# A bidirectional RWKV-7 scan with VectorE's turns written out, u copied by ScalarE and products taken with the decayed state, and attention's value products issued in one row

## The chip, the cores and the metric

The kernel runs on one core of a Trainium2 chip. A core has five engines that each work through their own list of instructions in order: TensorE (PE in the profile) for matrix products, VectorE (DVE), ScalarE (ACT), GpSimd (POOL) and SyncE (SP), which here issues most of the DMA transfers. They meet by semaphores. The metric is the device time of one execution in microseconds (us), lower is better. Before the change it is 1709.98 us, the median of three runs from 1708.64 to 1715.86.

## The reference

One encoder layer over 1024 tokens with a model width of 1024. The part that matters is this (shapes are noted behind):

```python
proj = rms_norm(x) @ w_in                      # q, k, v | r, k, v, ... of the time mix | branch gates
attn = windowed_gqa(q, k, v, sink)             # blocks of 128 queries, up to 3 key blocks each, 2 kv heads x 4 q heads
def step(state, inp):                          # time mix: two directions, 8 heads, state 64 x 64
    sa = einsum('dbhij,dbhj->dbhi', state, a_t)
    state = state * w_t[..., None, :] + sa[..., :, None] * b_t[..., None, :] + v_t[..., :, None] * k_t[..., None, :]
    y = einsum('dbhij,dbhj->dbhi', state, r_t)
rw = groupnorm(y_forward + flip(y_backward)) ...
merged = gate0 * (attn @ w_up_attn) + gate1 * (rw @ w_up_rwkv)
x = x + merged @ w_out
x = x + square(relu(rms_norm(x) @ w_ff1)) @ w_ff2
x = x + (p @ w_ple) * sigmoid(rms_norm(x) @ w_ple_gate)
```

All of it is float32. Where the kernel wants float32 accuracy from faster products it splits both operands into a high and a low part and takes three products (high by high, low by high, high by low); `split` (L197, L198) makes the parts: ScalarE casts the high one, VectorE subtracts for the low one.

## The kernel before

The program runs in stages: input projection and preparation (to about 340 us), attention (about 340 to 486 us), the scan (about 486 to 800 us), the epilogue and the branches' up products (to about 907 us), output projection, the two feed-forward products and the gated embedding.

**Attention** takes the 1024 queries in 8 tiles n of 128. For each tile and each of 2 kv heads it computes scores `sc`, a softmax, transposes the probabilities (`pt`, copied into `pT`), and at last the value products `po` (L956): for each key block j and each kv head, one product whose 64 output columns lie in that head's half of the array. Tiles 1 to 6 have three key blocks and so six products, tiles 0 and 7 two and four. Here, TensorE's order among independent work is left to the scheduler. Work of the input projection for the gates (`gmm`) fills TensorE between these products.

**The scan** is chunked: the 1024 tokens are 16 chunks of 64, and step s handles chunk s forward and chunk 15-s backward at once. Within a chunk the recurrence needs the inverse of a unit lower triangular matrix per head and direction; the kernel computes these inverses for blocks of NB = 4 steps together, one block ahead of their use. So inverse b (b = 1, 2, 3) is worked on during steps 4(b-1) to 4b-1. Its parts are:

- `low_products`: four parts (ci = 0 to 3), one for each chunk of the block, each 32 small products `lps` from loaded tiles `la` and `lb`, copied to `lt`. Loads of part ci+1 are issued when part ci has been computed.
- `inverse`: four ScalarE copies into `Lc` (1024 columns by 32 partitions each), a transposition `Lp` on VectorE, and 31 elimination steps of two VectorE operations each (`tmp`, a product, and `Z`, an addition).
- `inverse_turned`: two more transpositions `Zn` and `Zt`, and `inverse_off`: products `qps`, copies `Q`, and the off-diagonal part; the results go into `zi`.

Step s itself runs on TensorE in a fixed order (every product goes through `mmo`, L220, or is pinned): `carried(s)`, products of the operands with the state of step s-1 into `wy`; products for s+2 (`gps`, masked by VectorE into `gm`); `u_part`: `ups` = inverse by W, and next to it `wa` for the next step; `s_part`: `sps`, the contribution to the state; `y_part`: the outputs, again into `wy`; `operands(s+1)`: transpositions `tmps`, copied by ScalarE to `tm`. Eight gaps are filled with projection products (`gmm`) in steps 0 to 13, and `aside(i)` takes part i of the next inverse's low products in steps 0, 4 and 8. From step 12 on, the epilogue is mixed in.

The other engines' share of a step: u has 64 rows for each direction, on two halves of the partitions. VectorE copies the first half out of `ups` into `UV`, ScalarE the second (L1212, L1213). `W` of the next step is copied from `wa` by ScalarE (L1192) and VectorE adds the carried part (L1199). VectorE adds `sps` to the decayed old state (`S`, L1225) and decays it for the next addition (`Sc`, L1230). The state that `carried` multiplies is the undecayed `S`; the decay is put into the operands instead: `decayed` lets ScalarE scale the tiles `ra` in place, eight operations a step (L1164).

Only TensorE's order is fixed by hand. On VectorE and ScalarE a scheduler sets the order of the scan's work, so the elimination steps of the inverse stand wherever it placed them between `UV`, `W`, `gm`, `S`. DMA issues on SP stand in one list too: among them `g_d` (a gate tile that ScalarE has just made, `gth`, stored), `la` and `lb`, and, from step 11 on, `atl` and `wust` (attention's output and the weights that lift it), whose parts `aTh`, `aTl`, `wuhi`, `wulo` feed `uaps`.

Of the kernel before, what the change touches and what calls it, by code (L numbers as in the profile page):

```python
# [17 lines left out]
P = 128  # L18
# [6 lines left out]
NP = 4  # L25
# [38 lines left out]
LEAD = 1  # L64
FILLQ = 8

LOW_AT = 3
# [77 lines left out]
def block_kernel(ctx: ExitStack, tc: tile.TileContext, I: dict, out: bass.AP):  # L145
# [629 lines left out]
    def low_products(pl, ps_of, b, mm, behind=None):  # L775
# [14 lines left out]
        for ci in range(NB):  # L790
            la, lb = nxt
            pss = [ps_of([P, NP, 64], "lps") for _ in range(2)]
            for j in range(NP):
                for q in range(2):
                    for d in range(ND):
                        e = q ^ d
                        rows = slice(64 * e, 64 * e + 64)
                        l_, r_ = (lb, la) if d == 0 else (la, lb)
                        mm(pss[e][own[d], j, :], l_[d][rows, j, :], r_[d][rows, j, :], start=True, stop=True)
            for e in range(2):  # L800
                nc.scalar.copy(lt[:, 8 * ci + e:8 * ci + 8:2, :], pss[e])
            if ci + 1 < NB:
                nxt = load(ci + 1)
            yield lt
# [84 lines left out]
    with ExitStack() as s2:  # L889
# [21 lines left out]
        for n in range(NT):  # L911
# [42 lines left out]
            for j in range(nk):  # L954
                for kv in range(2):
                    nc.tensor.matmul(po[kv * 64:kv * 64 + 64], V[:, k0 + j, kv * 64:kv * 64 + 64], pTs[kv][:, j, :, :], start=(j == 0), stop=(j == nk - 1))  # L956
# [152 lines left out]

    ch_tm, ch_uv, ch_S, ch_wy, Sc = {}, {}, {}, {}, {}  # L1110

# [9 lines left out]
    def products(s, hf):  # L1121
# [14 lines left out]
        for e in range(2):  # L1136
            nc.vector.tensor_tensor(
                out=gm[hf][:, s % NB, e].rearrange("p (a b) t -> p a b t", b=2), in0=pss[e][:, 0:6].rearrange("p (a b) t -> p a b t", b=2),
                in1=gmask.unsqueeze(2).broadcast_to([P, 3, 2, 64]), op=ALU.mult)

# [17 lines left out]

    def decayed(s):

        for d in range(ND):
            for j in range(NP):
                r_ = ra_t[s % NRA, d][:, j, :]
                nc.scalar.activation(out=r_, in_=r_, func=AF.Copy, scale=Dt[:, d, j, s - 1:s])  # L1164

    def w_own(s, h, wa):
# [28 lines left out]
    def w_sum(s, W):  # L1195

        if s > 0:
            for e in range(2):
                nc.vector.tensor_tensor(out=W[:, e::2, :], in0=W[:, e::2, :], in1=ch_wy[s][e][:, 0:4, :], op=ALU.add)  # L1199

    def u_part(s, W):

        up = PB.tile([P, NH, 64], F32, name="ups", tag="us", bufs=1)
        nxt = s + 1 < NCH
        wa = wa_tile() if nxt else None
        for h in (0, 2, 4, 6, 1, 3, 5, 7):
            for d in range(ND):
                mmo(up[own[d], h, :], zi[own[d], 8 * (s % NB) + h, :], W[own[d], h, :], start=True, stop=True)
            if nxt:
                w_own(s + 1, h, wa)  # L1210
        UV = ch_uv[s]
        nc.vector.tensor_copy(UV[own[0], 0], up[own[0]])  # L1212
        nc.scalar.copy(UV[own[1], 1], up[own[1]])  # L1213
        return w_copy(wa) if nxt else None

    state = [None]

    def s_part(s):
        sp = PB.tile([P, ND, NP, 64], F32, name="sps", tag="us", bufs=1)
        for d in range(ND):  # L1220
            for h in range(NH):
                mmo(sp[own[h % 2], d, h // 2, :], ch_tm[s, d][:, h, :], ch_uv[s][:, d, h, :], start=True, stop=True)
        S = ch_S[s] = B.tile([P, ND, NP, 64], F32, name="S", bufs=2)
        if s > 0:
            nc.vector.tensor_tensor(out=S, in0=sp, in1=Sc.pop(s - 1), op=ALU.add)  # L1225
        else:
            nc.vector.tensor_copy(S, sp)
        if s < NCH - 2:
            Sc[s] = B.tile([P, ND, NP, 64], F32, name="Sc")
            state[0] = nc.vector.tensor_tensor(out=Sc[s], in0=S, in1=Dt[:, :, :, s].unsqueeze(3).broadcast_to([P, ND, NP, 64]), op=ALU.mult)  # L1230

    def y_part(s):
# [8 lines left out]
        for e in range(2):  # L1241
            yo = yv[:, e::2, c0:c1 + 1:c1 - c0, :]
            yp = ch_wy[s][e][:, 4:8, :].rearrange("q (d a) t -> q a d t", d=2)
            if s < NCH // 2:
                nc.scalar.copy(yo, yp)
            else:
                for d in range(ND):
                    nc.vector.tensor_tensor(out=yo[:, :, 1 - d], in0=yo[:, :, 1 - d], in1=yp[:, :, d], op=ALU.add)

    def low(b):  # L1250

        if b in lows:
            lts[b] = next(lows[b])

# [35 lines left out]
    for s in range(NCH):  # L1290
# [8 lines left out]
        def aside(i):  # L1299

            b = s // NB + 1
            if b < NCH // NB and (s % NB, i) in ((0, 0), (0, 1), (0, 2), (0, 3)):
                low(b)
                if i == 3:
                    zzs[b] = inverse(BI, lts[b])
            if ep is not None:
# [639 lines left out]
```

## Time and profile before

The profiled execution took 1708.72 us, 1.3 us less than the median; its span is 1706.9 us, so 1.8 us lie around the span.

| what | value |
|---|---|
| time, median of 3 (range) | 1709.98 us (1708.64 to 1715.86) |
| profiled execution, span | 1708.72 us, 1706.9 us |
| TensorE busy in the span | 1622.9 us, 95% |
| VectorE, ScalarE busy | 1146.3 us (67%), 869.2 us (51%) |
| attention, 340 to 486 us: TensorE, VectorE busy | 130.55 us, 103.34 us of 146 |
| scan, 486 to 800 us | 16 steps |

The busy shares of the whole span say little of the scan: there TensorE has gaps, and these are read from the waits. In the lists of waits the first name is the waiting operation, the name behind the arrow what it waited for; then follow the total in us, how often, and the longest. In the timelines the columns are start, duration, engine, line, operation, result and operands, and in brackets the idle time before with what ended it. Line L220 is the helper through which nearly all of the scan's products go, so the scan is read by tile names.

### The profile page before, as it was taken

To read this page: it belongs to the slowest core of one execution; us is meant where nothing else is said; L and a number is where in the kernel's file an instruction comes from. 1 tells how busy PE (TensorE), PEld (TensorE's weight loads), DVE (VectorE), ACT (ScalarE), POOL (GpSimd) and SP (SyncE) were. 2 spreads that over 40 slices of the span, in tenths; PEclk is the share of its full clock that TensorE was granted. 3 is DMA by queue.
4 is the path that set the end of the run, shared out by engine and by line. 5 is a ranking of instruction groups with operands and counts; after the bars stand their busy time and mean duration, and the time that the engine had idled before them with its cause. 6 is when DMAs were issued, how large, how long until landed. Compare 5 with 4: busy or idle time off the path is not lost.

```text
span 1706.9 us, 31260 instructions
## 1 busy us (share of the span) xinstructions
PE 1622.9 (95%) x12280; PEld 1310.1 (77%) x12280; DVE 1146.3 (67%) x2071; ACT 869.2 (51%) x1605; POOL 102.6 (6%) x113
## 2 busy tenths in 40 slices
PE   7999999989998988798999999999999999999998
PEld 7987777756567777676778878888888888888887
DVE  6658998165957596866764787676667867685342
ACT  5548887367645646565422454444444444544221
POOL 3430000411200000000000000000000000000000
PEclk9999999989999999899999999999999999999999
DMA  6353566755356544546762144444439865474110
GB/s 220 81 153 106 161 182 179 226 162 143 99 162 175 158 150 138 174 126 210 240 216 86 62 159 155 142 154 151 162 129 345 281 217 155 158 219 149 43 40 37
DMA packets 200835, 269.24 MB, mean 158 GB/s; under 512 B 47728, under 2 KB 103920, under 8 KB 200688
## 3 DMA queue, kind: packets, MB, share of 16 engines
q1 hardware_dynamic: 190752, 254.14, 47.0%
q0 software_dynamic: 9792, 12.59, 2.8%
q8 instruction: 96, 1.57, 0.4%
q10 hardware_dynamic: 144, 0.52, 0.1%
q14 instruction: 51, 0.42, 0.1%
HBM read 186.45 MB, written 80.74 MB: 157 GB/s over the span
## 4 chain that ended last, share of the span: by engine, by line
PE 72%; DVE 13%; DMA 7%; ACT 4%; issue 3%; POOL 1%; SPq 1%; DVEq 0%; ACTq 0%; POOLq 0%
PE ff1ps L1575 16%; PE ff2ps L1827 16%; PE gmm L220 2%; PE uaps L220 2%; DVE Z L824 2%; DVE tmp L821 2%; PE plps L230 2%; PE plps L228 2%; PE plps L226 2%; PE mm L238 2%; PE po L956 2%; PE mm L240 2%; PE mm L239 2%; DMA wst<-in_w_col_dram 1%; PE sc L927 1%
## 5 line engine op out<-in xcount | busy, mean ns | idle before, releaser
L1827 PE MATMUL ff2ps<-tl,sh 128*128 128x512 f32 x448 | 174.5, 390 | 0.2 <-DVE tl L198 0.2
L1827 PE MATMUL ff2ps<-th,sl 128*128 128x512 f32 x448 | 174.4, 389 | 0.0
L1827 PE MATMUL ff2ps<-th,sh 128*128 128x512 f32 x448 | 173.9, 389 | 0.0
L197 ACT CAST sh<-sst 128x512 fp32r<-128x512 f32 x109 | 67.8, 622 | 105.0 <-PE ff2ps L1827 49.4
L198 DVE TENSOR_TENSOR sl<-sst,sh 128x512 fp32r<-128x512 f32 x109 | 75.1, 689 | 46.4 <-ACT sh L197 46.3
L1575 PE MATMUL ff1ps<-mh,w1h 128*128 128x512 f32 x256 | 100.3, 392 | 1.9 <-ACT w1h L197 1.9
L1575 PE MATMUL ff1ps<-ml,w1h 128*128 128x512 f32 x256 | 99.9, 390 | 0.0
L1575 PE MATMUL ff1ps<-mh,w1l 128*128 128x512 f32 x256 | 99.6, 390 | 0.0
L1827 PEld LDWEIGHTS ff2ps<-tl,sh 128*128 128x128 f32 x448 | 84.1, 188 | 18.4 <-DVE tl L198 0.8
L1827 PEld LDWEIGHTS ff2ps<-th,sh 128*128 128x128 f32 x448 | 84.0, 188 | 17.8 <-ACT th L197 0.3
L1827 PEld LDWEIGHTS ff2ps<-th,sl 128*128 128x128 f32 x448 | 84.1, 188 | 17.3
L197 ACT CAST whi<-wst 128x512 fp32r<-128x512 f32 x100 | 60.2, 616 | 63.5 <-DMA wst<-in_w_col_dram 29.2
L197 ACT CAST w1h<-w1st 128x512 fp32r<-128x512 f32 x48 | 28.3, 620 | 95.2 <-DMA w1st<-in_w_ff_dram 58.3
L182 POOL TENSOR_TENSOR rstd<-ms,neghalf 128x1 f32<-128x1 f32 x24 | 14.8, 617 | 1029.1 <-DVE pp L198 573.1
L198 DVE TENSOR_TENSOR w1l<-w1st,w1h 128x512 fp32r<-128x512 f32 x48 | 31.7, 687 | 50.5 <-ACT w1h L197 50.5
L198 DVE TENSOR_TENSOR wlo<-wst,whi 128x512 fp32r<-128x512 f32 x72 | 48.2, 687 | 21.1 <-ACT whi L197 20.9
L226 PE MATMUL gmm<-hh,whi 128*128 128x512 f32 x136 | 56.7, 417 | 3.3 <-ACT whi L197 3.3
L1575 PEld LDWEIGHTS ff1ps<-mh,w1h 128*128 128x128 f32 x256 | 48.0, 188 | 12.9 <-ACT w1h L197 2.8
L1575 PEld LDWEIGHTS ff1ps<-mh,w1l 128*128 128x128 f32 x256 | 48.1, 188 | 10.8 <-DVE w1l L198 0.6
L228 PE MATMUL gmm<-hl,whi 128*128 128x512 f32 x136 | 56.2, 413 | 0.0
L1575 PEld LDWEIGHTS ff1ps<-ml,w1h 128*128 128x128 f32 x256 | 48.1, 188 | 10.0
L230 PE MATMUL gmm<-hh,wlo 128*128 128x512 f32 x136 | 55.6, 410 | 0.0
(397 smaller groups left out, 4585.4 us busy)
## 6 DMA issues: line engine op xcount, KB each, us to landing
wst<-in_w_col_dram SPq DMA_DIRECT2D x92, 256.0 KB, 3.4
tst<-in_w_ff_dram SPq DMA_DIRECT2D x80, 256.0 KB, 4.0
w1st<-in_w_ff_dram SPq DMA_DIRECT2D x32, 512.0 KB, 4.9
hid_S<-h SPq DMA_DIRECT2D x64, 256.0 KB, 2.1
sst<-hid_S SPq DMA_DIRECT2D x64, 256.0 KB, 3.1
hid_A<-h SPq DMA_DIRECT2D x48, 256.0 KB, 2.2
sst<-hid_A SPq DMA_DIRECT2D x45, 256.0 KB, 3.6
ra_d<-ra SPq DMA_DIRECT2D x8, 1024.0 KB, 5.7
```

What stands on the lines that cost most here:

```text
L197: a = nc.scalar.copy(hi, src)
L198: b = (lo_eng or nc.vector).tensor_tensor(out=lo, in0=src, in1=hi.bitcast(F32), op=ALU.subtract)
L220: tc.keep_in_program_order(nc.tensor.matmul(*a, **kw))
L226: mm(ps, ah, bh, start=(i == 0), stop=False)
L228: mm(ps, ah, bl, start=False, stop=False)
L230: mm(ps, al, bh, start=False, stop=(i == n - 1))
L238: nc.tensor.matmul(ps, ah, bh, start=(i == 0), stop=False)
L239: nc.tensor.matmul(ps, ah, bl, start=False, stop=False)
L240: nc.tensor.matmul(ps, al, bh, start=False, stop=(i == n - 1))
L821: nc.vector.tensor_tensor(out=tv, in0=Lp[:, t + 1:32, t:t + 1].broadcast_to([P, n, m]), in1=Z[:, t:t + 1, 0:m].broadcast_to([P, n, m]), op ...
L1575: nc.tensor.matmul(ps, x_[:, k, :], y_[:, k, :], start=start and k + i == 0, stop=k == 3 and i == 2, skip_group_check=True)
L1827: nc.tensor.matmul(banks[bs][i], x_[:, isl], y_, start=fresh and p + j == 0, stop=p == NPR - 1 and j == 2, skip_group_check=True)
```

## The change

It has five parts.

1. **Turns.** The scheduler no longer sets the order of VectorE's own scan work. `turn` pins each of these operations to the place where the program issues it: the mask products `gm`, the additions to `W`, `S`, `Sc`, `y`, and the operations of the inverse, which is now a generator (`inverse_steps`) advanced by `inverse_turn(n)`. `TURNS` gives the number of elimination steps at three places of each of the four steps of a block. What `split` issues (`wlo`, `aTl`, `wulo`, `rwl`) is not pinned, and neither is ScalarE's work.
2. **u** is copied out of `ups` by ScalarE alone, both halves.
3. **Decay.** `decayed` is gone; `carried` multiplies the decayed state `Sc` with the operands as loaded. In step 0 no copy of the state is made; `Sc` is taken from `sps`.
4. **Low products.** The copies into `Lc` are made part by part after each `lt` (32 partitions by 256 columns, sixteen for an inverse, instead of four of 1024 columns), and the fourth part, `aside(3)`, is moved from the end of the step (behind gap 7) to just behind gap 4, in steps 0, 4 and 8; the order of directions within a part is turned round.
5. **Attention.** The order of the two kv heads in the value products is turned round: the head whose probabilities are ready last goes first.

The core of the diff:

```diff
+TURNS = ((0, 0, 4), (3, 2, 5), (3, 2, 5), (4, 3, 1))
...
-                    for d in range(ND):
+                    for d in (1, 0):
...
-                for kv in range(2):
+                for kv in (1, 0):
                     nc.tensor.matmul(po[kv * 64:kv * 64 + 64], V[:, k0 + j, kv * 64:kv * 64 + 64], pTs[kv][:, j, :, :], start=(j == 0), stop=(j == nk - 1))
...
+    def turn(ins):
+        tc.keep_in_program_order(ins)
...
-    def decayed(s):
-
-        for d in range(ND):
-            for j in range(NP):
-                r_ = ra_t[s % NRA, d][:, j, :]
-                nc.scalar.activation(out=r_, in_=r_, func=AF.Copy, scale=Dt[:, d, j, s - 1:s])
...
-            S = ch_S[s - 1]
+            S = Sc[s - 1]
...
-        nc.vector.tensor_copy(UV[own[0], 0], up[own[0]])
-        nc.scalar.copy(UV[own[1], 1], up[own[1]])
+        for d in range(ND):
+            turn(nc.scalar.copy(UV[own[d], d], up[own[d]]))
...
-        S = ch_S[s] = B.tile([P, ND, NP, 64], F32, name="S", bufs=2)
+        S = sp
         if s > 0:
-            nc.vector.tensor_tensor(out=S, in0=sp, in1=Sc.pop(s - 1), op=ALU.add)
-        else:
-            nc.vector.tensor_copy(S, sp)
-        if s < NCH - 2:
-            Sc[s] = B.tile([P, ND, NP, 64], F32, name="Sc")
-            state[0] = nc.vector.tensor_tensor(out=Sc[s], in0=S, in1=Dt[:, :, :, s].unsqueeze(3).broadcast_to([P, ND, NP, 64]), op=ALU.mult)
+            S = B.tile([P, ND, NP, 64], F32, name="S", bufs=1)
+            turn(nc.vector.tensor_tensor(out=S, in0=sp, in1=Sc.pop(s - 1), op=ALU.add))
+        Sc[s] = B.tile([P, ND, NP, 64], F32, name="Sc", bufs=2)
+        turn(nc.vector.tensor_tensor(out=Sc[s], in0=S, in1=Dt[:, :, :, s].unsqueeze(3).broadcast_to([P, ND, NP, 64]), op=ALU.mult))
...
+    def low(b, ci):
+
+        lt = lts[b] = next(lows[b])
+        if ci == 0:
+            Lcs[b] = BI.tile([P, 32, 32], F32, name="Lc", tag="inv", bufs=3)
+        for r0 in range(0, P, 32):
+            k = r0 // 32 % 2
+            nc.scalar.copy(Lcs[b][r0:r0 + 32, 8 * ci:8 * ci + 8], lt[r0:r0 + 32, 8 * ci:8 * ci + 8, 32 * k:32 * k + 32])
...
+    def inverse_steps(b):
+
+        Lc = Lcs.pop(b)
+        Lp = BI.tile([P, 32, 32], F32, name="Lp", tag="inv", bufs=3)
+        turn(nc.vector.transpose(out=Lp, in_=Lc.rearrange("s p t -> s t p")))
...
+        for t in range(31):
+            n, m = 31 - t, t + 1
+            tv = tmp[:, 0:n * m].rearrange("p (n m) -> p n m", m=m)
+            turn(nc.vector.tensor_tensor(
+                out=tv, in0=Lp[:, t + 1:32, t:t + 1].broadcast_to([P, n, m]),
+                in1=Z[:, t:t + 1, 0:m].broadcast_to([P, n, m]), op=ALU.mult))
+            turn(nc.vector.tensor_tensor(out=Z[:, t + 1:32, 0:m], in0=Z[:, t + 1:32, 0:m], in1=tv, op=ALU.add))
+            yield
+        Zn = BI.tile([P, 32, 32], F32, name="Zn", tag="inv", bufs=3)
+        Zt = BI.tile([P, 32, 32], F32, name="Zt", tag="inv", bufs=3)
+        turn(nc.vector.transpose(out=Zn.rearrange("r p c -> r c p"), in_=Z.rearrange("p r c -> p c r")))
+        turn(nc.vector.transpose(out=Zt.rearrange("c p r -> c r p"), in_=Z))
+        zzs[b] = Zn, Zt, None
+
+    inv = [iter(())]
+
+    def inverse_turn(n):
+        for _ in range(n):
+            next(inv[0], None)
...
         gap(0)
         aside(0)
+        inverse_turn(TURNS[s % NB][0])
         gap(1)
         W = u_part(s, W)
-        if nxt:
-            decayed(s + 1)
         if more:
             products(s + 2, 1)
+        inverse_turn(TURNS[s % NB][1])
         gap(2)
         gap(3)
         aside(1)
         if nxt:
             s_part(s)
         y_part(s)
-        if s % NB == NB - 1 and s // NB < 3:
-            b = s // NB + 1
-            zzs[b] = inverse_turned(BI, zzs[b], state[0])
         aside(2)
         gap(4)
+        if s % NB == 0 and s // NB < 3:
+            aside(3)
+            inv[0] = inverse_steps(s // NB + 1)
+        inverse_turn(TURNS[s % NB][2])
         gap(5)
...
-        aside(3)
+        if s % NB or s // NB >= 3:
+            aside(3)
```

How this moves instructions is shown at three places. The first is TensorE in step 4, at the low products of block 2: `lps` are these products, `gmm` the filler, `tmps` the transpositions of the next step's operands. Before, from the last product of the third part to the first of the fourth:

```order
L220 MATMUL lps<-lb,la 64x64
L220 MATMUL gmm<-hh_90,wlo 128x512
L220 MATMUL gmm<-hh_90,whi 128x512
L220 MATMUL gmm<-hl_91,whi 128x512
...
L1154 MATMUL tmps<-ident,bkc_4614 128x128 x4
L1154 MATMUL tmps<-ident,bkc_4618 128x128 x4
...
L220 MATMUL gmm<-hh_90,wlo 128x512
L220 MATMUL lps<-la,lb 64x64
```

and now:

```order
L221 MATMUL lps<-la,lb 64x64
L221 MATMUL gmm<-hh_90,wlo 128x512
L221 MATMUL gmm<-hh_90,whi 128x512
L221 MATMUL gmm<-hl_91,whi 128x512
L221 MATMUL lps<-lb,la 64x64
```

Of the ten `gmm` and eight `tmps` that stood between the two parts, three `gmm` are left; the other seven and the `tmps` come behind the fourth part.

The second place is ScalarE in step 11, the last step before the epilogue. `gth` is the gate tile, `rac` are the tiles that `decayed` scales, `aTh` and `wuhi` high parts of loaded tiles. Before:

```order
L328 ACTIVATE gth<-gmm 128x512
L1192 COPY W<-wa 128x512
L1213 COPY UV<-ups 64x512
L1164 ACTIVATE rac_3037<-rac_3037,Dt 128x128 x2
L1164 ACTIVATE rac_3040<-rac_3040,Dt 128x128 x2
L197 CAST aTh<-atl 128x512 x2
L1156 COPY tm<-tmps 128x512
L197 CAST wuhi<-wust 128x512
L1156 COPY tm<-tmps 128x512
L197 CAST wuhi<-wust 128x512
```

and now:

```order
L329 ACTIVATE gth<-gmm 128x512
L1190 COPY W<-wa 128x512
L198 CAST aTh<-atl 128x512 x2
L198 CAST wuhi<-wust 128x512 x2
L1211 COPY UV<-ups 64x512 x2
L198 CAST aTh<-atl 128x512 x2
L198 CAST wuhi<-wust 128x512
```

The copies of u, which stood ahead of the casts of loaded tiles, now stand behind four of them.

The third place is VectorE in the same step. `tmp` and `Z` are the elimination steps of the inverse (the last three of them are left out at the mark), `aTl` and `wulo` low parts of the loaded tiles, `gm` the masked products. Before, where the elimination had ended ahead of the step:

```order
L1137 TENSOR_TENSOR gm_4610<-gps,gmask 128x384 x2
L1225 TENSOR_TENSOR S<-sps,Sc 128x512
L1230 TENSOR_TENSOR Sc<-S,Dt 128x512
L198 TENSOR_TENSOR aTl<-atl,aTh 128x512
...
L198 TENSOR_TENSOR wulo<-wust,wuhi 128x512
L198 TENSOR_TENSOR wulo<-wust,wuhi 128x512
L831 STREAM_TRANSPOSE Zn<-Z 128x32x32
```

and now:

```order
L199 TENSOR_TENSOR wulo<-wust,wuhi 128x512 x2
L1267 TENSOR_TENSOR tmp<-Lp,Z 128x175
L1270 TENSOR_TENSOR Z<-Z,tmp 128x7x25
...
L199 TENSOR_TENSOR wulo<-wust,wuhi 128x512
L1270 TENSOR_TENSOR Z<-Z,tmp 128x5x27
...
L1142 TENSOR_TENSOR gm_4610<-gps,gmask 128x384 x2
...
L1222 TENSOR_TENSOR S<-sps,Sc 128x512
...
L1224 TENSOR_TENSOR Sc<-S,Dt 128x512
...
L1274 STREAM_TRANSPOSE Zn<-Z 128x32x32
```

Seven elimination steps, the second `gm`, `S`, `Sc`, `y` and `Zn` now stand behind `aTl` and `wulo`, three of the latter among them.

More of the change, by code (lines that the diff above doesn't have):

```diff
@@ L1198, in w_sum @@
             for e in range(2):
[L1199 removed]
+                turn(nc.vector.tensor_tensor(out=W[:, e::2, :], in0=W[:, e::2, :], in1=ch_wy[s][e][:, 0:4, :], op=ALU.add))
     def u_part(s, W):
@@ L1247, in y_part @@
                 for d in range(ND):
[L1248 to L1253, printed above, removed]
+                    turn(nc.vector.tensor_tensor(out=yo[:, :, 1 - d], in0=yo[:, :, 1 - d], in1=yp[:, :, d], op=ALU.add))
+    Lcs = {}
+    def low(b, ci):
[9 more added lines that the diff above has]
+        turn(nc.vector.transpose(out=Lp, in_=Lc.rearrange("s p t -> s t p")))
+        Z = BI.tile([P, 32, 32], F32, name="Z", tag="inv", bufs=3)
+        nc.gpsimd.memset(Z, 0.0)
+        nc.gpsimd.memset(Z.rearrange("p r c -> p (r c)")[:, ::33], 1.0)
+        tmp = BI.tile([P, 256], F32, name="tmp", bufs=1)
+        for t in range(31):
+            n, m = 31 - t, t + 1
+            tv = tmp[:, 0:n * m].rearrange("p (n m) -> p n m", m=m)
+            turn(nc.vector.tensor_tensor(
+                out=tv, in0=Lp[:, t + 1:32, t:t + 1].broadcast_to([P, n, m]),
[11 more added lines that the diff above has]
+            next(inv[0], None)
     def begin_low(b):
@@ L1302, in aside @@
             if b < NCH // NB and (s % NB, i) in ((0, 0), (0, 1), (0, 2), (0, 3)):
-                low(b)
-                if i == 3:
-                    zzs[b] = inverse(BI, lts[b])
+                low(b, i)
             if ep is not None:
```

6 lines of the change are left out of this document (2 added, 4 removed).

## The prediction

> **What bounds the kernel now.** I read the page first, then the busy times by stage, then TensorE's waits in the scan, and last the timelines around the longest of them.
>
> ```profile
> span 1706.9 us, 31260 instructions
> PE 1622.9 (95%) x12280; PEld 1310.1 (77%) x12280; DVE 1146.3 (67%) x2071; ACT 869.2 (51%) x1605; POOL 102.6 (6%) x113
> ```
>
> TensorE sets the time; outside it only 84 us are left. The change leaves its products as they are, so it can win only idle time, or time in which an array half stands empty. Where is the idle time?
>
> ```profile
> 430.00:475.00 45.00, 40.77 (x198) 25.32 (x196) 40.90 (x139) 29.83 (x82) 8.73 (x7) 1.00 0.27 82
> 475.00:600.00 125.00, 114.42 (x2601) 93.62 (x2601) 76.48 (x155) 69.15 (x151) 2.22 (x4) 0.97 0.62 175
> 527.00:537.00 10.00, 6.75 (x83) 5.94 (x82) 9.59 (x27) 5.17 (x12) 0.00 (x0) 0.83 0.58 142
> 600.00:720.00 120.00, 99.50 (x2340) 82.26 (x2340) 97.31 (x230) 63.58 (x139) 1.11 (x2) 0.97 0.50 151
> 707.00:717.00 10.00, 4.03 (x120) 3.75 (x116) 8.92 (x14) 6.88 (x13) 0.00 (x0) 0.74 0.86 259
> 720.00:800.00 80.00, 69.44 (x1134) 52.73 (x1133) 53.29 (x101) 43.66 (x79) 0.00 (x0) 0.92 0.51 161
> ```
>
> Columns: stretch, length, busy TensorE, weight loads, VectorE, ScalarE, GpSimd, granted clock, DMA share, GB/s. From 475 to 800 us TensorE lacks 10.6 + 20.5 + 10.6 = 41.7 us of 325. VectorE is nearly full exactly where TensorE is emptiest. The waits from 486 to 910 us:
>
> ```profile
> PE sps L220 <- ACT UV L1213: 13.8, 8, 3.3
> PE qps L220 <- ACT aTh L197: 6.0, 1, 6.0
> PE wy L220 <- DVE y L1248: 2.2, 4, 0.7
> PE ups L220 <- DVE W L1199: 1.8, 5, 0.5
> PE lps L220 <- DMA lb<-bk_d: 1.5, 1, 1.5
> PE gps L220 <- DVE gm L1137: 0.4, 1, 0.4
> ```
>
> The largest is `sps` on u. In step 5 it looks so (VectorE, ScalarE, TensorE):
>
> ```profile
> 602.17 0.30 DVE L824 TENSOR_TENSOR Z<-Z,tmp 128x135 f32<-128x135 f32 x1
> 602.38 0.68 DVE L1212 COPY UV<-ups 64x512 f32<-64x512 f32 x1
> 603.09 0.58 ACT L1213 COPY UV<-ups 64x512 f32<-64x512 f32 x1 [3.78 <-DVE UV L1212]
> 771.83 1.15 PE L220 MATMUL sps<-UV,tm 128*64 128x64 f32 x32 [1.69 <-ACT UV L1213]
> ```
>
> VectorE's half of u stands behind five elimination steps, and ScalarE's half starts only when VectorE's has ended. ScalarE had stood idle for 3.78 us.
>
> **The change part by part.** The sum is made against the profiled execution, 1708.7 us (1.3 below the median).
>
> *Waits in steps 1 to 10.* With both halves of u on ScalarE no elimination step stands ahead of them; two copies take 2 x 0.58 us against 0.68 + 0.58 in series now. Of the 13.8 us, 1.69 lie at 772 us (the last row above) and 0.40 in step 11 (below); 11.7 us go. Of the waits on `W`, `y` and `gm` (1.8 + 2.2 + 0.4 = 4.4) I take 0.6 as lying behind step 10; 3.8 go, since `turn` puts `W`, `gm` and `y` ahead of the elimination steps. Together **-15.5**. The cover is ScalarE, which also loses the scaling of `ra`:
>
> ```profile
> L1164 ACT ACTIVATE rac<-rac,Dt 128x128 f32<-128x128 f32 x120 | 38.9, 392 | 25.1 <-PE gps L220 24.7
> L811 ACT COPY Lc<-lt 32x1024 f32<-32x1024 f32 x12 | 12.5, 1045 | 0.2
> ```
>
> That is 38.9 us over 15 steps, 2.6 a step, off a half-busy engine: by itself worth nothing on TensorE, but it keeps u's copies, `tm` and `gth` from queueing. The twelve `Lc` copies become 48 of a quarter's width. No row has that shape; between a quarter of 1045 ns and the 0.58 us of u's 512 columns I take 0.37, 1.5 us a part, still hidden, since ScalarE is at 55% (69.15 of 125); uncovered, 48 x 0.37 less the 12.5 of now would be 5 us.
>
> *VectorE as pacemaker.* Pinning does not shorten VectorE's other work, so what TensorE no longer waits for in u it can meet elsewhere.
>
> ```profile
> L821 DVE TENSOR_TENSOR tmp<-Lp,Z 128x252 f32<-128x252 f32 x6 | 2.5, 422 | 0.2
> L1225 DVE TENSOR_TENSOR S<-sps,Sc 128x512 f32<-128x512 f32 x14 | 9.6, 686 | 4.6 <-PE sps L220 4.6
> L1137 DVE TENSOR_TENSOR gm<-gps,gmask 128x384 f32<-128x384 f32 x62 | 32.3, 550 | 15.2 <-PE gps L220 15.2
> L1248 DVE TENSOR_TENSOR y<-y,wy 128x128 f32<-128x128 f32 x32 | 7.7, 281 | 0.4 <-PE wy L220 0.4
> 706.84 1.10 PE L220 MATMUL wy<-gm,UV 128*64 128x64 f32 x32
> 707.88 1.09 PE L1154 MATMUL tmps<-ident,bkc 128*128 128x128 f32 x8
> ```
>
> Between `sps` and the next `W`, VectorE now has `S`, `Sc` (2 x 0.69) and five elimination steps (10 x 0.42 in the middle of an inverse), 5.6 us. TensorE has meanwhile `wy` of the outputs 1.1, `tmps` 1.1, the carried products (32 of the same kind, 1.1) and ten fillers, whose rows start 0.24 us apart (587.02 and 587.26 in the next fence): 5.7. So it is about even: some 0.3 us of wait a block. In steps 3 and 7 `Zn` (2.0) stands behind the last elimination step, `S`, `Sc` and (step 7) four `y` of 0.28, with `qps` behind it; there I take 1.1 and 1.4 us. With half a microsecond in step 10 this is about **+4**, with 0 and +6 as ends.
>
> *The fourth part of the low products.* It moves ahead, but its loads do not:
>
> ```profile
> 588.11 0.62 SPq L782 DMA_DIRECT2D lb<-bk_d  x1
> 587.02 0.40 PE L220 MATMUL gmm<-hh,whi 128*128 128x512 f32 x1
> 587.26 0.40 PE L220 MATMUL gmm<-hl,whi 128*128 128x512 f32 x1
> 591.91 0.24 PE L220 MATMUL lps<-lb,la 64*64 64x64 f32 x1 [1.50 <-DMA lb<-bk_d]
> ```
>
> In step 4 the last load is issued at 588.11, behind the store of `g_d`, and its product starts at 591.91 after 1.50 us of waiting; two products of the part had run by then, so TensorE had come to it at about 590.1. After the change it comes right behind the `gmm` of 587.26, at about 587.5: 2.6 us earlier. ScalarE makes `gth`, hence the store and the loads, perhaps 0.7 us sooner (a group of `rac` of 1.3 us gone, 0.58 of u come). In step 4 this makes a wait of about 3.4 us. Each of the three blocks waits 2.6 - 0.7 = 1.9 us more: **+5.6** (ends: 0, if the loads come as much earlier as the products; +7.8 if not at all). In step 4 a wait stands there already, so nothing absorbs it.
>
> *Step 11.* Here the queues decide.
>
> ```profile
> 708.59 1.24 ACT L197 CAST aTh<-atl 128x512 fp32r<-128x512 f32 x2 [1.48 <-DMA atl<-at_d]
> 711.50 0.62 ACT L197 CAST wuhi<-wust 128x512 fp32r<-128x512 f32 x1
> 712.15 0.69 DVE L198 TENSOR_TENSOR wulo<-wust,wuhi 128x512 fp32r<-128x512 f32 x1 [0.22 <-ACT wuhi L197]
> 712.76 2.04 DVE L831 STREAM_TRANSPOSE Zn<-Z 128x1024 f32<-128x1024 f32 x1
> 705.86 1.15 PE L220 MATMUL sps<-UV,tm 128*64 128x64 f32 x32 [0.40 <-ACT UV L1213]
> 714.94 3.62 PE L220 MATMUL qps<-Zn,lt 32*32 32x32 f32 x128 [5.97 <-ACT aTh L197]
> 713.26 0.53 SPq L1000 DMA_DIRECT2D wust<-in_w_up_attn_dram  x1
> ```
>
> Now `Zn` already stands behind two `aTl` and two `wulo`, and `qps` waits 5.97 us, until `Zn` ends at 714.8 (the listed releaser had long ended). After the change u's copies stand behind `aTh` x2 and `wuhi` x2: they start at 712.1, not 704.5; `sps` at 713.3, not 705.9. On VectorE seven elimination steps, `gm`, `S`, `Sc` and `y` stand behind loaded tiles too, the third `wulo` among them, whose `wust` is issued at 713.26 now and may land at 715 to 716 if it is issued sooner. From a third `wulo` ending at 717: nine elimination operations of 0.2 to 0.3 (2.4), two `gm` 1.1, `S` and `Sc` 1.4, four `y` 1.1, `Zn` 2.0 make 725, against 714.8. Operations on VectorE overlap a little (`Zn` starts at 712.76, while `wulo` of 712.15 is listed to 712.84), for which I take off 0.8: **+9.4**; ends 0 (tiles landed before they are asked for) and +11.
>
> *Steps 12 to 15*: the 1.69 us on u at 772 us may go, u may queue behind other casts: **-1** (0 to -1.7).
>
> *Attention.* The value products:
>
> ```profile
> 381.82 1.07 PE L956 MATMUL po<-pT,V 128*64 128x512 f32 x2
> 391.02 2.79 PE L956 MATMUL po<-pT,V 128*64 128x512 f32 x10
> ```
>
> The profile counts each product twice. The first of six stands alone, 1.07 us with half the array empty; the five others alternate halves and take three slots, 2.79. With the head order turned round, all six come when the last probabilities are there, in three slots: 1.07 us less in each of 8 tiles, 8 us at most. Filler covers the first while TensorE is full; in the last three tiles VectorE (40.90 of 45) limits, and the product's early place was itself free filler. Five tiles at 1 us: **-5** (0 to -8).
>
> Sum: -15.5 + 4 + 5.6 + 9.4 - 1 - 5 = **-2.5**, so 1706.2 in the profiled execution's terms, **1707.5** as a median.
>
> The granted clock adds a doubt: around the longest wait on u, 3.3 us in step 1, it was 0.83 from 527 to 537, and 0.74 around step 11. The Trainium skill's page "TensorE: Matmul & The Clock Gate", section "What's actually happening", says that about 3.4 us of idle time halve the clock; the trace agrees in direction. By it, the wait of step 4 would be at the limit and cost a stretch at half speed besides, while the one in step 1 costs none any more; by the row, which shows less than full speed after 3.3 us already, the two cancel, and the sum stays.
>
> **The rivals.**
>
> *Queues win (slower).* If step 11 costs its full 11, the loads gain nothing (+7.8), VectorE takes 6 and attention gives 1: -15.5 + 6 + 7.8 + 11 - 1 - 1 = +7.3; a clock of 0.83 over 10 us behind two waits of 3.5 us takes 1.7 each, +10.7: 1720.7. It is one mechanism, work tied to late DMA placed ahead of work that TensorE needs, in step 11 and at the low products, and it decides once both together cost over 20 us. For: the 5.97 us wait is already of this kind. Against: it needs nearly every end at once.
>
> *Step 11 mild (faster).* If the tiles land as soon as the casts ask, the 9.4 falls to 0: -11.9, 1698. For: DMA share is only 0.50 to 0.62 before. Against: it is 0.86 from 707 to 717, and the loads stand behind `g_d` in SP's list as before.
>
> *Attention gains in full, VectorE is no bound (faster)*: -15.5 + 5.6 + 9.4 - 1 - 8 = -9.5, 1700.5.
>
> *No effect of pinning*, the scheduler's order having been nearly as good: only attention and step 11 count, +4, 1714. Against: five elimination steps in front of u are in the trace.
>
> **How the numbers follow.** Less than 0.5%, 8.5 us, can't be told from no change here. My sum, within that, has a chance of 0.43, pinning without effect 0.07: same 0.50. Step 11 mild 0.20 and attention in full 0.12: faster 0.32. Queues 0.18: slower. The range, 1694 to 1719, reaches below the mild case by 4 and just to the slow one.
>
> **What would show it.** Right: `sps` waits for `UV` no more in steps 1 to 10; `ra` scaling gone; `lps` waits of 2 to 4 us on `lb` in steps 0, 4, 8; `sps` and `qps` of step 11 late by 7 and 10 us. Wrong: `sps` of step 11 without a wait, `W` or `Zn` waits over 6 us in sum, `po` still in four slots, or attention's end moved by nothing.

## The result and the profile after

The changed kernel takes 1697.3 us (median of 11 runs, 1694.52 to 1704.26), the kernel before 1709.98 us in the same number of runs. The ratio is 0.9933, 95% interval 0.9915 to 0.995: faster by 0.5 to 0.85%. That is 12.7 us, where 2.5 were forecast; the time lies in the stated range, and on the side to which I had given a chance of 0.32. Among the experiments below four single executions, of 3211 to 8857 us, stand far outside all others; the ratios leave them out, the medians hold them.

The first lines of the page after, and windows of the changed kernel (stretch, length, busy TensorE, weight loads, VectorE, ScalarE, GpSimd, granted clock, DMA share, GB/s):

```profile
span 1694.4 us, 31186 instructions
PE 1615.2 (95%) x12280; PEld 1311.1 (77%) x12280; DVE 1138.1 (67%) x2055; ACT 847.0 (50%) x1537; POOL 103.1 (6%) x113
```

```profile
430.00:475.00 45.00, 41.99 (x243) 28.65 (x241) 44.60 (x139) 31.49 (x86) 8.78 (x7) 1.00 0.30 97
517.00:527.00 10.00, 10.00 (x189) 8.29 (x190) 9.14 (x24) 4.02 (x8) 0.00 (x0) 1.00 0.71 186
527.00:537.00 10.00, 10.00 (x233) 8.08 (x233) 9.62 (x24) 4.45 (x8) 0.00 (x0) 1.00 0.65 205
600.00:720.00 120.00, 101.53 (x2454) 84.60 (x2456) 89.35 (x200) 52.85 (x103) 1.11 (x2) 0.90 0.47 143
686.00:696.00 10.00, 2.87 (x78) 2.74 (x79) 4.78 (x10) 4.73 (x8) 0.00 (x0) 0.79 0.81 252
696.00:706.00 10.00, 3.46 (x62) 3.02 (x60) 9.05 (x23) 4.50 (x8) 0.00 (x0) 0.67 0.61 198
```

The clock times of the two kernels don't match, since step 1 now comes 7 us and step 11 some 12 to 17 us earlier. The hole of step 1, at 527 to 537 before, is closed: from 517 to 537 TensorE is busy all the time, at full clock. The hole of step 11, at 707 to 717 before, lies at 686 to 706 now and has grown: TensorE is busy for 6.3 of these 20 us. TensorE's waits from 486 to 910 us in the changed kernel:

```profile
PE lps L221 <- DMA lb<-bk_d: 8.8, 3, 4.0
PE sps L221 <- ACT UV L1211: 7.4, 2, 6.6
PE uaps L221 <- ACT aTh L198: 5.5, 2, 4.8
PE qps L221 <- DVE Zn L1274: 4.9, 1, 4.9
PE tmps L1159 <- DVE gm L1142: 1.6, 1, 1.6
PE ups L221 <- DVE W L1197: 0.3, 1, 0.3
```

The eight waits of `sps` on u have become two, of 6.6 us in step 11 and 0.8 behind it; those on `W`, `y` and the scan's `gm` have gone but for 0.3 on `W` and the one of step 11. In their place the low products wait 8.8 us for `lb`, in steps 0, 4 and 8 (2.70, 2.13 and 3.95 us); before it was 1.5 us in step 4, and in step 8 0.8 us that the profile calls issue, a wait for nothing that it shows.

Where the time went is read from one product that both kernels have in every step, the first `sps`. In the kernel before, steps 0, 10, 12 and 14 (start, duration, engine, line, names):

```profile
512.57 0.34 PE L220 MATMUL sps<-UV,tm 128*64 128x64 f32 x4
693.56 0.28 PE L220 MATMUL sps<-UV,tm 128*64 128x64 f32 x2 [1.68 <-ACT UV L1213]
735.90 0.28 PE L220 MATMUL sps<-UV,tm 128*64 128x64 f32 x2
771.83 0.28 PE L220 MATMUL sps<-UV,tm 128*64 128x64 f32 x2 [1.69 <-ACT UV L1213]
```

and after the change:

```profile
503.69 0.28 PE L221 MATMUL sps<-UV,tm 128*64 128x64 f32 x2
676.59 0.28 PE L221 MATMUL sps<-UV,tm 128*64 128x64 f32 x2
723.32 0.28 PE L221 MATMUL sps<-UV,tm 128*64 128x64 f32 x2
757.90 0.28 PE L221 MATMUL sps<-UV,tm 128*64 128x64 f32 x2 [0.83 <-ACT UV L1211]
```

| stretch | before | after | difference | forecast |
|---|---|---|---|---|
| start to `sps` of step 0 (attention in it) | 512.57 | 503.69 | -8.9 | -5 |
| step 0 to step 10 | 180.99 | 172.90 | -8.1 | -5.9 (-15.5 + 4 + 5.6) |
| step 10 to step 12 (step 11 in it) | 42.34 | 46.73 | +4.4 | +9.4 |
| step 12 to step 14 | 35.93 | 34.58 | -1.4 | -1 |
| step 14 to the span's end | 935.1 | 936.5 | +1.4 | 0 |
| span | 1706.9 | 1694.4 | -12.5 | -2.5 |

Up to step 14 every stretch moved the way it was forecast; three sizes were off. One execution of each kernel was profiled, and among the runs below those with the same program in a stretch differ by up to 4.9 us ahead of step 0 (503.85 and 508.71), up to 5.5 us in steps 0 to 10 (172.9 and 178.4) and up to 1.9 us from step 10 to step 12 (46.7 and 48.6), so a smaller difference between two runs is not shown by its stretch alone.

In step 11 the queues did what the order had shown. VectorE, with rows left out at the marks:

```profile
690.76 0.69 DVE L199 TENSOR_TENSOR aTl<-atl,aTh 128x512 fp32r<-128x512 f32 x1 [4.58 <-ACT aTh L198]
...
692.40 1.45 DVE L199 TENSOR_TENSOR wulo<-wust,wuhi 128x512 fp32r<-128x512 f32 x2
693.77 0.33 DVE L1267 TENSOR_TENSOR tmp<-Lp,Z 128x175 f32<-128x175 f32 x1
...
697.50 0.68 DVE L199 TENSOR_TENSOR wulo<-wust,wuhi 128x512 fp32r<-128x512 f32 x1
...
701.28 0.68 DVE L1222 TENSOR_TENSOR S<-sps,Sc 128x512 f32<-128x512 f32 x1
...
703.39 2.05 DVE L1274 STREAM_TRANSPOSE Zn<-Z 128x1024 f32<-128x1024 f32 x1
```

VectorE stands idle for 4.58 us at the first `aTl`, with seven elimination steps behind it that need nothing from it. ScalarE does the same with u:

```profile
690.12 0.62 ACT L198 CAST aTh<-atl 128x512 fp32r<-128x512 f32 x1 [2.50 <-DMA atl<-at_d]
691.75 1.37 ACT L198 CAST wuhi<-wust 128x512 fp32r<-128x512 f32 x2
693.03 1.17 ACT L1211 COPY UV<-ups 64x512 f32<-64x512 f32 x2
```

### The profile page after: what moved, and what is told of

It reads as the page before. It is cut to its first block, busy times and chain, and to the rows that moved or that the text cites. A ratio compares the mean times of both kernels' runs of the same rounds, so it can differ in the third digit from the quotient of the medians.

```text
span 1694.4 us, 31186 instructions
## 1 busy us (share of the span) xinstructions
PE 1615.2 (95%) x12280; PEld 1311.1 (77%) x12280; DVE 1138.1 (67%) x2055; ACT 847.0 (50%) x1537; POOL 103.1 (6%) x113
## 4 chain that ended last, share of the span: by engine, by line
PE 74%; DVE 11%; DMA 6%; ACT 4%; issue 3%; POOL 1%; SPq 0%; DVEq 0%; ACTq 0%; POOLq 0%
PE ff2ps L1856 17%; PE ff1ps L1604 16%; PE gmm L221 4%; PE uaps L221 2%; PE plps L231 2%; PE plps L229 2%; PE plps L227 2%; PE mm L239 2%; PE mm L241 2%; PE mm L240 2%; PE gps L221 1%; DMA wst<-in_w_col_dram 1%; DMA g1t<-g_d 1%; PE mmo L241 1%; PE mmo L239 1%
```

## The experiments

Eleven kernels were run. A time is the median of its runs, a ratio that to the kernel before, with its 95% interval; "the change" is 0.9933 (0.9915 to 0.995).

**Attention's row alone.** The kernel before with this edit:

```diff
-                for kv in range(2):
+                for kv in (1, 0):
```

> The kernel before with one edit: the order of the two kv heads in attention's value products. In the trace of the change the scan's first product that waits for VectorE's mask stands at 476.6 us against 484.5, so theory A (the row of six saves a slot of about 1 us in all 8 tiles) expects -8 us, a ratio of 0.995, and TensorE's waits on smk falling from 5.0 to about 1.5. The rival, my prediction's term (five tiles, the rest hidden behind VectorE), expects -5 us and the waits unchanged or longer.

Measured: 1706.29 us, 0.9975 (0.9955 to 0.9994). TensorE's waits in attention in this run:

```profile
PE sc L927 <- DVE mx L928: 4.0, 6, 1.3
PE pt L948 <- DVE smk L945: 2.2, 4, 0.8
```

The value products of a tile now run in one row. In the changed kernel, which has the same edit (the profile counts each product twice):

```profile
403.42 2.79 PE L957 MATMUL po<-pT,V 128*64 128x512 f32 x12
```

All six take the 2.79 us that five took before, and the 1.07 us of the first one alone are gone. With this edit alone, too, no tile has a separate first product left. The time falls by 4.3 us (1 to 8), and the scan's first `qps` starts at 485.1 us against 490.3: 5 us, the prediction's size, not theory A's 8. The `smk` waits fall from 5.0 to 2.2, as theory A had it, but waits on `mx`, another of VectorE's operations, rise from 0.9 to 4.0: VectorE takes back part of what TensorE saves. The other direction gives more:

**The change without attention's row.** Only that line put back.

> The changed kernel with the old order of the kv heads in the value products. By the kernel before with the new order alone (about 5 us at the scan's start) the time rises by 5 us, to 1702; if the order of the products is what makes all 8 us at the scan's start, by 8, to 1705. If the pins on gm at the scan's start make the missing 3 us, the first qps stands 3 us earlier than in the kernel before (487 against 490.3).

Measured: 1706.72 us, 0.9976 (0.9958 to 0.9993), 9.4 us above the change. The first `qps` starts at 489.0 us, close to the kernel before, so the pins make little of the 8 us at the scan's start (482.2 against 490.3). By `sps` of step 0 the row is worth 10.5 us here (514.2 against 503.7) and 5.9 in the kernel before (506.7 against 512.6). Whether the row gains 4 or 9 us the intervals do not settle: both hold 3 to 8.

**u on ScalarE alone.** The kernel before, with the scheduler's order and this edit:

```diff
-        nc.vector.tensor_copy(UV[own[0], 0], up[own[0]])
-        nc.scalar.copy(UV[own[1], 1], up[own[1]])
+        for d in range(ND):
+            nc.scalar.copy(UV[own[d], d], up[own[d]])
```

> The kernel before with both halves of u copied by ScalarE, VectorE's order left to the scheduler. Theory B (u's copy behind elimination steps is the whole loss of steps 1 to 10) expects the 13.8 us of sps waits on u to fall under 2, and -10 to -12 us, ratio 0.993. The rival (VectorE is the pacemaker, its order must be pinned for it) expects waits on W, gm and y to grow by what u loses: -2 to -4 us, ratio 0.998 to 0.999.

Measured: 1710.39 us, 1.0002 (0.9982 to 1.0022): no gain. The waits of this run from 486 to 910 us:

```profile
PE ups L220 <- DVE W L1199: 4.6, 3, 2.1
PE wy L220 <- issue: 4.2, 3, 2.3
PE gmm L220 <- issue: 3.6, 1, 3.6
PE wy L220 <- DVE y L1248: 2.9, 3, 2.2
```

The waits on u fall from 13.8 to 1.4 us. Waits on VectorE's results take part of their place (`W` from 1.8 to 4.6, `y` from 2.2 to 2.9, `S` from nothing to 1.8), and so do waits called issue; steps 0 to 10 take 183.8 us, against 181.0 before. The profiled execution took 1716.66 us, 6.3 above the median, so these sums may be on the high side. Theory B falls: removing the largest wait alone gains nothing, because TensorE then waits for other things, the next results of VectorE first.

**The change without its pins.** `turn` returns without pinning; all else stays. The diff passes u's two copies on ScalarE through `turn` as well, so these are pinned in the changed kernel, and here they are not.

```diff
     def turn(ins):
-        tc.keep_in_program_order(ins)
+        return ins
```

> The changed kernel with only the pins on VectorE and ScalarE taken away; the program issues everything in the same places. If the pins carry the gain of steps 1 to 10, elimination steps go ahead of W and gm again and the waits on W, y, gm come back: +4 to +8 us against the change, ratio to the kernel before 0.996 to 0.998. If the moves alone carry it: within 2 us of the change, ratio 0.993.

Measured: 1702.14 us, 0.9945 (0.9923 to 0.9966), 4.8 us above the change. The stretches tell more than the sum. In this run steps 0 to 10 take 184.3 us (`sps` at 505.0 and 689.3), 11.4 more than in the change, with waits on `Sc`, `y`, `Z` and `W` in them; but step 10 to step 12 takes 37.8 us, 8.9 less than in the change. The fixed order gains 11.4 us up to step 10 and gives 8.9 of it back in step 11. There, without pins, ScalarE copies u at 702.0 us, ahead of the first cast at 704.2, and `sps` waits 0.3 us, so the wait of 6.6 us is gone with the pins. A kernel with pins on VectorE alone was not run.

**u by halves, pinned.** The change with u's first half on VectorE again.

```diff
-        for d in range(ND):
-            turn(nc.scalar.copy(UV[own[d], d], up[own[d]]))
+        turn(nc.vector.tensor_copy(UV[own[0], 0], up[own[0]]))
+        turn(nc.scalar.copy(UV[own[1], 1], up[own[1]]))
```

> The changed kernel with u's first half copied by VectorE again, pinned at its place. If it is the queue on VectorE that made u late, and not the engine, the pinned copy stands ahead of the elimination steps of its step and waits at most for those pinned before it: sps waits of 0 to 1 us a step, the time 0 to 5 us above the change, 1697 to 1702. If the engine matters (VectorE as pacemaker has 0.7 us a step less): 7 to 11 us above, 1704 to 1708.

Measured: 1702.65 us, 0.9964 (0.995 to 0.9977), 5.4 us above the change, at the edge of the first case. The longest wait lies in step 11 (TensorE, then VectorE and ScalarE):

```profile
706.17 1.97 PE L221 MATMUL sps<-UV,tm 128*64 128x64 f32 x32 [14.92 <-ACT UV L1211]
704.83 0.68 DVE L1210 COPY UV<-ups 64x512 f32<-64x512 f32 x1
705.54 0.58 ACT L1211 COPY UV<-ups 64x512 f32<-64x512 f32 x1 [2.18 <-DVE UV L1210]
```

`sps` waits 14.92 us there, and the four others of its waits make 4.2 together, 2.5 of them in steps 1 to 10, where they were 11.7 in the kernel before. Steps 0 to 10 take 174.7 us against 172.9. So where VectorE's order is fixed, its half of u costs hardly 2 us over ten steps: u was late by its place in the queue far more than by its engine. The long wait of step 11 is mostly made good behind it, since step 10 to step 12 takes 49.0 us against 46.7. Where the rest of the 5.4 us lies, these stretches don't settle.

**The decay put back.** The change with `decayed` and the undecayed state again:

```diff
+    def decayed(s):
...
-            S = Sc[s - 1]
+            S = ch_S[s - 1]
...
+        if nxt:
+            decayed(s + 1)
```

> The changed kernel with the decay put back into the operands: ScalarE scales ra (2.6 us a step), and the carried products use the undecayed state. My prediction held the scaling to be worth nothing by itself: within 2 us of the change. The rival: ra operations stand ahead of u's copies and gth on ScalarE, sps waits for u come back at 0.5 to 1 us a step and the lps waits grow by 0.7 each: 1702 to 1708.

Measured: 1703.01 us, 0.9964 (0.9949 to 0.998), 5.7 us above the change. By the time that is the rival's case, though the waits of `sps` in steps 1 to 10 did not come back; I had called the scaling worth nothing by itself. It costs 5.7 us, though ScalarE is half idle. Where, the traces show less surely: steps 0 to 10 take 176.7 us against 172.9, no more than single executions scatter; the `lps` waits are 10.3 us against 8.8, and `sps` of step 11 waits 8.5 us against 6.6. Both hang on ScalarE's list, `lb` by the store of `gth` ahead of its load, so the likely reason is that the scaling stands ahead of what TensorE waits for.

**The low products put back.** The fourth part, the inverse's start and its first four elimination steps at the end of steps 0, 4 and 8 again:

```diff
-        if s % NB == 0 and s // NB < 3:
-            aside(3)
-            inv[0] = inverse_steps(s // NB + 1)
-        inverse_turn(TURNS[s % NB][2])
+        if s % NB or s // NB >= 3:
+            inverse_turn(TURNS[s % NB][2])
...
-        if s % NB or s // NB >= 3:
-            aside(3)
+        aside(3)
+        if s % NB == 0 and s // NB < 3:
+            inv[0] = inverse_steps(s // NB + 1)
+            inverse_turn(TURNS[s % NB][2])
```

> The changed kernel with the fourth part of the low products, and with it the inverse's start and its first four elimination steps, put back to the end of steps 0, 4 and 8. Theory C (the earlier place costs what my sum said) expects the lps waits on lb to fall from 8.8 us to about 2.5 and the time by 5 to 6 us: ratio 0.990. The rival (VectorE starts the inverse later and TensorE waits for W behind it instead) expects W waits of 1 to 2 us in each of steps 1, 5, 9 and the time within 2 us of the change: ratio 0.993.

Measured: 1699.02 us, 0.9925 (0.9897 to 0.9953): the same as the change. The 8.8 us of waits on `lb` are gone, and this stands in their place:

```profile
PE ups L221 <- DVE W L1197: 7.1, 4, 3.0
```

In step 1 of this run `W` is added at 520.8 us, behind `Lp`, which starts at 516.6, and four elimination steps. The earlier place costs its wait and saves this one. As a price of the move, +5.6 was right for the wait and left out the other side.

**Loads two parts ahead, and casts later.** Two edits that take away the two losses, each alone and both together, on the changed kernel. First the loads, with six buffers instead of four:

```diff
...
-        nxt = load(0)
+        nxt = [load(0)] if behind else [load(0), load(1)]
...
-            la, lb = nxt
+            la, lb = nxt.pop(0)
+            if not behind and ci + 2 < NB:
+                nxt.append(load(ci + 2))
...
```

> The changed kernel with la and lb loaded two parts ahead instead of one (six buffers each instead of four), so that the last loads stand ahead of g_d in SP's list. Theory C (the 8.8 us of lps waits on lb are lost time) expects them to go and -6 to -9 us against the change, about 1690. The rival, which the run with the low products put back speaks for (VectorE is the pacemaker in the steps behind), expects waits on W or gm to take their place: within 3 us of the change.

Measured: 1696.89 us, 0.992 (0.9896 to 0.9945), the same as the change. The scan's waits on `lb` are gone, and 2.1 us of `tmps` on `lt` have come in their place: steps 0 to 10 take 166.0 us against 172.9. But in its profiled execution the scan's first `qps` came 3.7 us and step 0's `sps` 5 us later than in the change, and step 10 to step 12 took 1.9 us more. The delay ahead of step 0 is scatter: the run with both edits has the same program up to there and does not show it. Second, the tiles of attention's up products are asked for later:

```diff
         for h in range(2):
             hs = slice(512 * h, 512 * h + 512)
+            if h == 0:
+                for _ in range(17):
+                    yield 1
...
-                for _ in range(BRIDGE):
+                for _ in range(BRIDGE - 17):
```

> The changed kernel with attention's output tiles and the first up weights (atl, wust and their parts) asked for 17 filler places later in the program, nothing else; on ScalarE u of step 11 then stands ahead of their casts, on VectorE the elimination, S, y and Zn ahead of wulo. Theory D (these parts, queued ahead, cost step 11 its time) expects the waits of sps (6.6 us) and tmps (1.6) of step 11 to go and qps to be reached about 8 us earlier, of which uaps gives some back because its parts come later: -4 to -8 us against the change, 1690 to 1693. The rival (step 11 is bound by the landing of those tiles whatever stands in the queues) expects uaps to wait for what sps and qps no longer wait for: within 2 us of the change.

Measured: 1695.14 us, 0.9911 (0.9888 to 0.9935): 2.2 us below the change, within the intervals and less than the 4 to 8 expected. From step 10 to step 12 it takes 40.1 us, against 46.7 in the change and 42.3 before: u's wait there falls from 6.6 to 0.5 and that of `tmps` is gone, `qps` waits 6.2 us instead of 4.9, and `uaps` does not wait more (4.8 us in all against 5.5). In the profiled execution 4 us were lost between steps 3 and 4, among others 2.8 in a wait called issue. The rival's reading, that the landing of the tiles bounds step 11, falls.

**Both edits together.**

> Both edits together: the deeper loads and the later casts. If the two gains are separate, they add: -10 to -15 us against the change, 1682 to 1687. If VectorE's work between step 8 and Zn of step 11 is the bound, no more than the larger of the two, about 1690.

Measured: 1686.54 us, 0.9859 (0.9836 to 0.9881), 10.8 us below the change and clear of it, as expected if the gains add: the whole is 1.4% faster than the kernel before. Steps 0 to 10 take 167.5 us, step 10 to 12 38.7. Its waits:

```profile
PE qps L221 <- DVE Zn L1279: 5.3, 1, 5.3
PE uaps L221 <- ACT aTh L198: 4.1, 2, 3.4
PE tmps L1164 <- ACT lt L804: 2.1, 3, 0.7
PE sps L221 <- ACT UV L1216: 1.2, 2, 0.8
```

By the stretches the two gains add (5.4 and 8.0 us); by the medians each alone shows less than its stretch, 0.4 and 2.2 us, and why, the four runs of each leave open.

**Zn ahead of S.** On this kernel, the last of `qps`' waits:

```diff
-TURNS = ((0, 0, 4), (3, 2, 5), (3, 2, 5), (4, 3, 1))
+TURNS = ((0, 0, 4), (3, 2, 5), (3, 2, 5), (4, 4, 0))
```

> The kernel with deeper loads and later casts, and the last place of the table of turns changed from (4, 3, 1) to (4, 4, 0): Zn and Zt stand ahead of S, Sc and y in steps 3, 7 and 11. There qps of step 11 still waits 5.3 us for Zn. If S, Sc and y, queued ahead of Zn, make that wait (0.7 + 0.7 + 1.1 us, and what they wait for), it falls to 1 to 3 us and the time by 2 to 4 us against that kernel, to 1683 or 1684. The rival: S now stands behind 4 us of transposition, and the carried products of the next step wait for Sc: no gain, 1686 to 1688.

Measured: 1688.9 us (1682.3 to 1689.47), 0.9891 (0.9874 to 0.9907). The wait falls to 2.9 us in the profiled execution, which is the fastest of its four runs at 1682.3; the other three lie at 1688.8 to 1689.5. No gain is shown.

## Why the prediction was right or wrong

The forecast was no change, 1707.5; what came was a gain of 12.7 us. The mechanisms were the ones named, and up to step 14 each stretch moved the way it was forecast. The likeliest case, no change, failed by sizes. Three terms were forecast too slow: step 11 by 5.0 us, attention by 3.9 and VectorE as pacemaker by 4. All three miss to the same side, so that 1697.3 still lies in the range, 1694 to 1719, is owed to its width.

- *Waits in steps 1 to 10, -15.5.* Right as a count: 11.7 us on u and 2.9 on `W`, `y` and `gm` are gone there, -14.6. But the working put the gain down to u's copies by themselves ("with both halves of u on ScalarE no elimination step stands ahead of them"). u on ScalarE alone gained nothing (1.0002), u by halves in a fixed order lost hardly 2 us in these steps, and without the pins they take 184.3 us, no less than before. The pins carry it.
- *VectorE as pacemaker, +4.* This term failed. In steps 1 to 10 no wait on `W` is left, and none for `Zn` in steps 3 and 7; the 0.3 us on `W` lie at 754 us. VectorE can pace the scan, as the runs with u alone and with the low products put back showed, but in the order that `TURNS` fixes the work is even with TensorE's: I had counted 5.6 against 5.7 us and still charged a wait.
- *ScalarE's scaling, 0.* "By itself worth nothing" was wrong: put back, it costs 5.7 us. But it is no term that the sum lacks, since the waits above and below account for steps 0 to 10 without it. It is part of why they are gone, as the prediction said of u's copies, `tm` and `gth`. The 48 quarter copies, taken at 0.37 us, took 0.40.
- *The fourth low product, +5.6.* The waits rose from 2.3 to 8.8, +6.5, in each of the three steps between 2.1 and 4.0 us. Right as a wait. As a price it stood alone: put back, the same time returns as waits on `W`.
- *Steps 0 to 10 as a whole, -5.9.* Measured -8.1: the -14.6 and +6.5 above, 2.5 us less of waits called issue, and 2.4 us more of busy TensorE for the same products. The last two were not forecast, and that they cancel is luck.
- *Step 11, +9.4.* The largest miss. u started at 693.0, 16.4 us behind `sps` of step 10 where I had reckoned 18.5, behind the casts as the queue had it, and `sps` waited 6.6, `tmps` 1.6, `qps` 4.9, together 13.1 against 6.4 before. That is +6.7, not 9.4: I had reckoned `Zn` to end at 725 in the old time scale, 10 us late, and `qps` was 7.6 late (705.6 against 714.9, from a step 10 that was 17.0 earlier). `sps` was 5.4 late, not 7. What put u behind the casts is most likely its own pin, since without pins it stands ahead of them: the section on the change says that ScalarE's work is not pinned, but the diff has `turn` around u's copies. And 3.2 us came back behind it: from `qps` to `sps` of step 12 it took 17.7 us against 21.0, where the kernel before had run 10 us at a clock of 0.50 and a wait of 1.9 on issue. Net +4.4.
- *Attention, -5.* By itself 5.1 us at the scan's start and 4.3 in the time, as predicted; in the change 8.9 to `sps` of step 0. The rival that gave it the full 8 had the size that came in the change. Its reason, that VectorE is no bound, does not show: VectorE was busy for 44.6 of 45 us in 430 to 475. Why the row gives more in the change than alone stays open.
- *Steps 12 to 15, -1*: -1.4.

Of the rivals, "Step 11 mild" lies nearest by its number, 1698 with a chance of 0.20, and a part of its reason holds: by `sps` of step 10 the first `aTh` was cast at 13.5 us instead of 15.0, so the tiles came somewhat sooner. But they did not land as soon as the casts asked (ScalarE waited 2.50 us), and step 11 still lost 4.4. "Attention gains in full, VectorE is no bound", 1700.5 with a chance of 0.12, had the size of both its terms. "No effect of pinning" is refuted: the pins are worth 11.4 us up to step 10, and 4.8 in the time. The slower rival's mechanism, work tied to late DMA ahead of what TensorE needs, is real, and with both its places mended the kernel falls to 1686.5. It decided less than that rival had it, since its waits in part replaced others: those on `lb` the ones on `W`, those of step 11 the 6.4 us of before.

The granted clock in two windows after the change, behind the wait of `qps`, and in one before it:

```profile
706.00:711.00 5.00, 5.00 (x125) 4.57 (x121) 4.90 (x7) 2.31 (x4) 0.00 (x0) 0.50 0.02 7
711.00:716.00 5.00, 4.96 (x207) 4.01 (x209) 2.12 (x5) 2.31 (x4) 0.00 (x0) 0.88 0.33 108
```

```profile
712.00:722.00 10.00, 7.06 (x153) 5.93 (x155) 9.74 (x12) 6.36 (x12) 0.00 (x0) 0.50 0.79 251
```

From step 10 to step 12 it gave no case against the change: over that stretch it was 0.84 before and is 0.82 now. In steps 0 to 10 it did, with 0.96 where it was 0.99. At the end of each of the three waits for `lb` lies a stretch at half speed: 0.50 over 511 to 514 us, 0.52 over 579 to 582 and 0.50 over 648 to 654. The kernel before had one such stretch there, at the end of the 3.3 us of step 1. The prediction had let one gained and one lost cancel; three came for one that went.

The Trainium skill's page "TensorE: Matmul & The Clock Gate", section "What's actually happening", has about 3.4 us of idle time halve the clock; behind the wait of 4.9 us the trace agrees, with 0.50 in the first window and 0.88 in the second, and behind the waits for `lb` of 2.70 and 2.13 us it does not, since less idle time was enough there.

TensorE is busy for 162.35 us in steps 0 to 10, against 159.93 before for the same products. With the loads two parts ahead it is 160.63 us at a clock of 0.99, with both edits 162.22 us at 0.98, so how much of the 2.4 us is the clock stays open.

## What to carry to other kernels

Price a removed wait by what is late next: where the engine waited for is itself nearly full, the largest row can fall to almost nothing without any gain, and here only an order that puts what TensorE needs first turned it into time. When work is pinned on one engine, look for work that waits for a transfer and is queued ahead of it: here seven elimination steps stood 4.6 us behind a subtraction whose data had not landed, u's copies stood behind four casts, and asking for that data 17 places later in the program, with the loads two parts ahead, was worth 10.8 us. An engine at 50% can still be on the path by its queue.

## What the runs showed that had not been expected

- ScalarE's scaling, 2.6 us a step on an engine half idle, was worth 5.7 us of time (1703.0 against 1697.3).
- At the end of each wait of 2 to 4 us for `lb` the granted clock was half for 3 to 6 us, so such a wait can cost more than itself.
- Two edits, each alone within the intervals of the change (1696.9 and 1695.1 against 1697.3), made 10.8 us together.
- TensorE's waits called issue, of up to 3.6 us, come in every profiled execution, and in each also at the carried products behind `qps`. What they are, no run here shows.
